# Scores of two attention heads issued together, their low-half passes on 64 rows each

## The chip, the cores and the metric

The kernel runs on one core of a Trainium2 chip. The metric is the time of one execution on the device, in microseconds (us). Differences of about 0.2% are what a measurement of this kernel can resolve.

## What is computed

One hybrid decoder layer over 512 tokens of width 1024 in float32: an mLSTM branch and a sparse-attention branch run in parallel on the normalised input, are merged by gates, and a gated convolution MLP follows. What matters here is the attention's selected and windowed part. With 8 query heads in 2 groups of 4, head width 64 and at most 8 selectable blocks of which 16 may be taken, both see all earlier keys, each with its own keys `ks`, `kw` and its own softmax:

```python
ps = masked_softmax(jnp.einsum('bghqd,bgqmd->bghqm', qb, ksel) * scale, smask)
o_slc = jnp.einsum('bghqm,bgqmd->bghqd', ps, vsel)
pw = masked_softmax(jnp.einsum('bghqd,bgkd->bghqk', qb, kwin) * scale, wmask)
o_win = jnp.einsum('bghqk,bgkd->bghqd', pw, vwin)
...
qk = jax.nn.silu(causal_dwconv(jnp.concatenate([mq, mk], axis=-1), m_conv_w, m_conv_b))
```

## The kernel before, in words

Matrix products with float32 accuracy are made of rounded float32 operands: each operand is split into a rounded high part and the low remainder, and a product is three passes, high by high, high by low and low by high. A pass is one TensorE instruction with its own weight load: up to 128 rows of contraction, 128 weight columns, 512 columns of the moving operand.

*Operands of the attention.* The head width is 64, so the array's 128 rows hold two things at once. `q_transposes` (L839) writes, for each head and each query tile of 128 tokens, a 128x128 block of `QS`: rows 0 to 63 the high part of q, rows 64 to 127 its low part (L850 subtracts on VectorE; L849 makes the rounded copy on ScalarE). The keys of both kinds stand twice, in rows 0 to 63 and again in 64 to 127, in `KKH` (high parts) and `KKL` (low parts).

*Scores.* `att_scores(i, h)` (L897) serves one head of query tile i, with n = i + 1 key tiles of 256 columns (both kinds). In blocks of up to 512 columns it issues the high pass (L906), on the last block the causal mask (L908), and the low pass (L909), all over 128 rows. One high pass so gives K_high times both parts of q, one low pass K_low times both. The scores go to `sp`, a tile of two PSUM banks, of which the pool has two (`psS`). VectorE then takes the maximum (L912).

*The rest of a head.* `att_exp` (L915) has ScalarE take the exponentials of the two kinds (L921) into a tile `P` of the pool `s4` (six slots); `att_scale` (L924) divides by the sum and multiplies by the gate on VectorE. `att_transposes` (L931) transposes up to four 128x128 blocks on TensorE into the only buffer `pt` and copies them back (L235 on VectorE or L233 on ScalarE, by the plan: in tile 3 the first four by VectorE, the second four by ScalarE; in tile 2 the other way round; tiles 0 and 1 have no second four). `att_pv` (L939) takes two heads and adds their outputs with passes of 64 weight columns (L947).

*The order* is written out by hand in `attention()` (L960): for the 32 (tile, head) pairs it issues the scores of the next head, then the transposes and, for odd heads, the output of the current one. At three points per head a `Filler` puts in work of the projections that remain (here `gm`, `mo`, `mqk`, `gn`: L488 to L490, three passes of 512 columns per step), by a budget in nanoseconds from the table `PLAN` (`f1`, `f2`, `f3`). For heads 4 to 7 the compressed branch of the next tile is put in at the end, and its output at the start of head 0. Each engine works its queue in the order of issue.

*The convolution.* `evac_conv` (L725) writes the convolved q and k of the mLSTM branch into `cv0` and `cv1`, two tiles of the pool `s4`; ScalarE starts each 512 columns and VectorE adds three taps (L732). The projection pages are 2048 columns wide, eight slots (`page`).

*The mLSTM part* that follows (`mls_s`, L1091) has passes over part of the rows: L1097 over rows 0 to 35, then L1105 to L1107 over 64 rows, the lower half for even heads, the upper half for odd ones.

Of the kernel before, what the change touches and what calls it, by code (L numbers as in the profile page):

```python
# [15 lines left out]
P = 128  # L16
# [112 lines left out]
def FL(key, default):  # L129
    return PLAN.get(key, default)  # L130
# [30 lines left out]
def body(ctx, tc, I, out, dbg=None):  # L161
# [26 lines left out]
    def sm(shape, name, bufs=2, dt=F32):  # L188
        return small.tile(shape, dt, name=name, tag=name, bufs=bufs)
# [16 lines left out]
    def s4(name, dt=F32):  # L206
        return ar.tile([P, 1024], dt, name=name, tag="s4", bufs=6)
# [4 lines left out]
    def psS(name):  # L212
        return ps.tile([P, 1024], F32, name=name, tag="s", bufs=2)
# [4 lines left out]
    def po(name):  # L218
        return ps.tile([P, 512], F32, name=name, tag="po", bufs=1)
# [503 lines left out]
        cp("e_mo", 0, T["mo"][:, m, :], a)  # L723

    def evac_conv(m, a):  # L725
        if m % 2 == 0:
            T[f"cv{m // 2}"] = s4(f"cv{m}")
        c = T[f"cv{m // 2}"][:, (m % 2) * 512:(m % 2) * 512 + 512]
        act.activation(c, a, AF.Identity, bias=col("m_conv_b", m), scale=col("m_conv_w", 12 + m))

        def tap(k):
            dve.scalar_tensor_tensor(c[:, k:], a[:, :S - k], col("m_conv_w", (3 - k) * 4 + m), c[:, k:],  # L732
                                     op0=ALU.mult, op1=ALU.add)
            if m == 3 and k == 3:
                done.add("CONV")

        for k in (1, 2, 3):
            after(k - 1, lambda k=k: tap(k))
# [88 lines left out]
    def qst(t):  # L827
        return T["QS"][t // 2][:, (t % 2) * 1024:(t % 2) * 1024 + 1024].rearrange("p (h c) -> p h c", h=8)
# [10 lines left out]
    def q_transposes(t, qdup):  # L839
        for hb in range(2):  # L840
            if hb:
                fill(FL("z6", 650))
            p = (po if hb else pt)(f"pq{t}{hb}")
            pv = p.rearrange("p (h c) -> p h c", h=4)
            for hh in range(4):
                h = hb * 4 + hh
                pe.transpose(pv[:, hh, :], qdup[:, h * P:(h + 1) * P], ident)
            d = qst(t)[:, hb * 4:hb * 4 + 4, :]
            act.activation(d, pv, AF.Copy)  # L849
            dve.tensor_sub(d[64:128], pv[64:128], d[64:128])  # L850

    def cmp_scores(i):
        q = qst(i)
        sp = psS(f"sc{i}")
        pe.matmul(sp[:, :512], identr, cmaskr[:, i:i + 1, :].to_broadcast([P, 8, 64]), start=True, stop=False)
        for h in range(8):
            pe.matmul(sp[:, h * 64:h * 64 + 64], q[:, h, :], kkc[:, h // 4].rearrange("p a n -> p (a n)"),
                      start=False, stop=(h == 7))
        sv = sp[:, :512].rearrange("p (h z n) -> p h z n", h=8, z=2)
        pc = vst[:, 1024:1792]  # L860
        raw = pc[:, 0:256].rearrange("p (h n) -> p h n", h=8)
        cp(f"e_sc{i}", 0, raw, sv[:, :, 1, :])
        s2 = pc[:, 256:512].rearrange("p (h n) -> p h n", h=8)
        dve.tensor_add(s2, sv[:, :, 0, :], raw)
        return pc
# [26 lines left out]
    def cmp_out(acc, pc):  # L892
        for pr in range(4):
            pe.matmul(acc[:, pr * P:(pr + 1) * P], vbd[:, pr // 2, pr % 2, :],
                      pc[:, 512 + (pr // 2) * P:512 + (pr // 2 + 1) * P], start=(pr == 0), stop=False)

    def att_scores(i, h):  # L897
        g = h // 4
        q = qst(i)[:, h, :]
        sp = psS(f"sp{i}_{h}")  # L900
        n = i + 1
        for b in range((n + 1) // 2):
            j1 = min(n, 2 * b + 2)
            w = (j1 - 2 * b) * 256
            o = sp[:, b * 512:b * 512 + w]
            pe.matmul(o, q, T["kkh"][:, g, 2 * b:j1].rearrange("p j y c -> p (j y c)"), start=True, stop=False)  # L906
            if j1 == n:
                pe.matmul(sp[:, i * 256:i * 256 + 256], identr, maskr, start=False, stop=False)  # L908
            pe.matmul(o, q, T["kkl"][:, g, 2 * b:j1].rearrange("p j y c -> p (j y c)"), start=False, stop=True)  # L909
        sv = sp[:, :n * 256].rearrange("p (j y c) -> p y j c", y=2, c=P)  # L910
        nmx = sm([P, 2], "nmx", 4)
        dve.tensor_reduce(nmx, sv, axis=AX.XY, op=ALU.max, negate=True)  # L912
        return sv, nmx

    def att_exp(i, h, sv, nmx):  # L915
        n = i + 1
        Pt = s4(f"P{i}_{h}")
        Pv = Pt[:, :n * 256].rearrange("p (j y c) -> p y j c", y=2, c=P)
        den = sm([P, 2], "aden", 4)
        for y in range(2):  # L920
            act.activation(Pv[:, y], sv[:, y], AF.Exp, bias=nmx[:, y:y + 1], accum_out=den[:, y:y + 1])  # L921
        return Pt, Pv, den

    def att_scale(i, h, Pv, den):  # L924
        gd = sm([P, 2], "agd", 4)
        dve.reciprocal(gd, den)
        dve.tensor_mul(gd, gd, gts[:, i, h * 3 + 1:h * 3 + 3])
        for y in range(2):
            (pool if FL(f"p_sc{i}{y}", 1) == 2 else dve).tensor_scalar(Pv[:, y], Pv[:, y], gd[:, y:y + 1], None, op0=ALU.mult)

    def att_transposes(i, h, b, Pt):  # L931

        nb = min(4, 2 * (i + 1) - 4 * b)
        p = pt(f"ptp{i}_{h}_{b}")
        for s in range(nb):
            pe.transpose(p[:, s * P:(s + 1) * P], Pt[:, (4 * b + s) * P:(4 * b + s + 1) * P], ident)  # L936
        cp(f"e_pt{i}{b}", 1 - b, Pt[:, b * 512:b * 512 + nb * P], p[:, :nb * P])

    def att_pv(i, h, PTs, acc):  # L939

        n = i + 1
        pr = h // 2
        for s in range(2 * n):
            j, y = s // 2, s % 2
            for z in range(2):
                g = (h + z) // 4
                pe.matmul(acc[z * 64:z * 64 + 64, pr * P:(pr + 1) * P], vv[:, y, j, g * 64:g * 64 + 64],  # L947
                          PTs[z][:, s * P:(s + 1) * P], start=False, stop=(h == 6 and s == 2 * n - 1))
# [9 lines left out]
        dve.tensor_sub(ol, av, oh)  # L958

    def attention():  # L960
        its = [(i, h) for i in range(NT) for h in range(8)]
        f1 = [FL(f"f1_{k}", v) for k, v in enumerate((1950, 1300, 1000, 1000)) for _ in range(8)]
        f2 = [FL(f"f2_{k}", v) for k, v in enumerate((0, 0, 1300, 1300)) for _ in range(8)]
        f3 = [FL(f"f3_{k}", v) for k, v in enumerate((650, 1000, 300, 300)) for _ in range(8)]
        pcs = {0: pc0}
        rows, step = rows_b(), None
        sv, nmx = att_scores(0, 0)
        Pt, Pv, den = att_exp(0, 0, sv, nmx)
        fill(FL("z7", 1950))
        att_scale(0, 0, Pv, den)  # L970
        acc = po("on0")
        cmp_out(acc, pcs[0])
        fill(FL("z9", 1300))
        for n, (i, h) in enumerate(its):
            nxt = its[n + 1] if n + 1 < len(its) else None
            if nxt:
                nsv, nnmx = att_scores(*nxt)
            fill(f1[n])
            if nxt and FL(f"q2_ex{i}", 0) == 0:
                nPt, nPv, nden = att_exp(*nxt, nsv, nnmx)  # L980
            if h == 0 and i:
                acc = po(f"on{i}")
                cmp_out(acc, pcs[i])
            nb = (i + 2) // 2
            att_transposes(i, h, 0, Pt)
            if nxt and FL(f"q2_ex{i}", 0) == 1:
                nPt, nPv, nden = att_exp(*nxt, nsv, nnmx)
            fill(f2[n])
            if nb > 1:
                att_transposes(i, h, 1, Pt)  # L990
            if nxt:
                att_scale(*nxt, nPv, nden)
            fill(f3[n])
            if h % 2:
                att_pv(i, h - 1, (prev, Pt), acc)
            prev = Pt
            if rows and n >= FL("q32_rb", 6) and (step != "R4" or h in (1, 2)):
                step = next(rows, "end")
                if step == "end":
                    rows = None  # L1000
                    done.add("ROWS")
            if i + 1 < NT:
                if h == 4:
                    pcs[i + 1] = cmp_scores(i + 1)
                elif h == 5:
                    cmp_exp(i + 1, pcs[i + 1])
                elif h == 6:
                    cmp_scale(i + 1, pcs[i + 1])
                elif h == 7:
                    cmp_transposes(i + 1, pcs[i + 1])  # L1010
            if h == 7:
                att_out(i, acc)
            if nxt:
                Pt, Pv, den = nPt, nPv, nden


    uoc = consts.tile([P, 40], F32, name="uoc")
# [634 lines left out]
```

## Time and profile before

| | |
|---|---|
| median of 3 runs | 787.01 us (786.48 to 788.13) |
| the profiled execution | 786.64 us, of which the span from the first to the last instruction is 784.8 us |
| TensorE matmul busy | 773.2 us (99% of the span) |
| TensorE weight loads busy | 640.5 us |
| VectorE, ScalarE, GpSimd busy | 466.5, 374.5, 211.3 us |
| the attention's scores to its last output | 120 to 276 us of the span |

Passes are pipelined: the bar of a pass is longer than the time it adds, so what a pass costs is read from one start to the next. In the time line each line is a start, a duration, the engine, the line of the kernel, the operation, the tile written and the tiles read, the form (rows*columns of the weights, then the moving operand), and in brackets how long the engine was idle before it and what it waited for.

### The profile page before, as it was taken

Reading aid. Unit: us, or ns where it says so; the run is one execution under the profiler, and the core shown is the slowest. Engines: PE = TensorE matmul, PEld = TensorE weight load, DVE = VectorE, ACT = ScalarE, POOL = GpSimd, SP = SyncE. Lnnn points to the kernel's source line nnn. Section 1 sums busy time; section 2 is a strip of 40 time slices with the busy share of each in tenths; the row PEclk is TensorE's granted clock in tenths of the full one; section 3 lists DMA queues with packets and bytes.
Section 4 is the critical chain, followed back from the end, with each engine's and each line's share of the span. In section 5 each row is a group of like instructions: output and inputs, shape, how many; then the busy total and the mean of one; then the engine's idle time right before and its main releaser. Section 6 shows DMA issues by size and latency. Waiting matters only on the chain.

```text
span 784.8 us, 10544 instructions
## 1 busy us (share of the span) xinstructions
PE 773.2 (99%) x4037; PEld 640.5 (82%) x4037; DVE 466.5 (59%) x823; ACT 374.5 (48%) x631; POOL 211.3 (27%) x221
## 2 busy tenths in 40 slices
PE   7999999999999999999999999999999999999998
PEld 5798778887888888888888988888888888888886
DVE  4576785677566754566627455545555454565865
ACT  6254536744665576475624253333433333455441
POOL 4420022121111113110110027755455443200700
PEclk9999999999999999999999999999999999999999
DMA  6984059756647466643588157664554534575472
GB/s 231 288 216 141 19 99 178 126 108 108 108 82 128 89 87 143 120 100 138 137 269 282 41 205 282 235 240 174 205 215 173 187 125 160 210 273 188 147 235 88
DMA packets 93892, 129.03 MB, mean 164 GB/s; under 512 B 6512, under 2 KB 72208, under 8 KB 92433
## 3 DMA queue, kind: packets, MB, share of 16 engines
q1 hardware_dynamic: 63054, 91.64, 35.0%
q0 software_dynamic: 30784, 36.70, 22.6%
q8 instruction: 32, 0.52, 0.3%
q14 instruction: 20, 0.16, 0.1%
q10 hardware_dynamic: 2, 0.00, 0.0%
HBM read 94.79 MB, written 15.73 MB: 141 GB/s over the span
## 4 chain that ended last, share of the span: by engine, by line
PE 90%; DVE 7%; ACT 2%; issue 1%; POOL 0%; DVEq 0%; POOLq 0%
PE ff L1368 10%; PE ff L1367 10%; PE ff L1369 10%; PE P L427 4%; PE P L428 4%; PE P L426 4%; PE on L947 2%; PE ptp L936 2%; PE wo L426 2%; PE wo L427 2%; PE wo L428 2%; PE gn L488 2%; PE gn L490 2%; PE gn L489 2%; PE gm L488 1%; PE gm L490 1%
## 5 line engine op out<-in xcount | busy, mean ns | idle before, releaser
L94 DVE TENSOR_TENSOR whl<-raw,whl 128x1024 fp32r<-128x1024 f32 (+1 forms) x108 | 136.5, 1276 | 148.7 <-ACT whl L88 148.7
L88 ACT ACTIVATE whl<-raw 128x1024 fp32r<-128x1024 f32 (+2 forms) x144 | 144.8, 1012 | 126.4 <-PE ff L1369 57.2
L1367 PE MATMUL ff<-h2H,whl 128*128 128x512 f32 (+1 forms) x384 | 142.8, 372 | 0.0
L1368 PE MATMUL ff<-h2L,whl 128*128 128x512 f32 (+1 forms) x384 | 142.6, 371 | 0.0
L1369 PE MATMUL ff<-h2H,whl 128*128 128x512 f32 (+1 forms) x384 | 142.6, 371 | 0.0
L92 POOL DMA_DIRECT2D whl<-raw x34 | 47.1, 1384 | 234.9 <-ACT whl L91 183.9
L1367 PEld LDWEIGHTS ff<-h2H,whl 128*128 128x128 f32 x384 | 72.3, 188 | 12.6
L1369 PEld LDWEIGHTS ff<-h2H,whl 128*128 128x128 f32 x384 | 72.3, 188 | 12.5
L1368 PEld LDWEIGHTS ff<-h2L,whl 128*128 128x128 f32 x384 | 72.4, 188 | 12.3
L921 ACT ACTIVATE P<-sp,nmx 128x128 f32<-128x128 f32 (+3 forms) x64 | 33.1, 524 | 36.9 <-DVE nmx L912 36.5
L1419 ACT ACTIVATE ct<-ct 128x512 f32<-128x512 f32 x22 | 13.9, 632 | 54.1 <-DVE ct L1417 54.1
L912 DVE TENSOR_REDUCE nmx<-sp 128x2 f32<-128x256 f32 (+3 forms) x32 | 26.2, 818 | 18.0 <-PE sp L909 17.9
L91 ACT ACTIVATE whl<-raw 128x1024 fp32r<-128x1024 f32 x34 | 35.7, 1049 | 0.0
L426 PE MATMUL P<-whl,g 128*128 128x512 f32 x88 | 34.2, 389 | 0.0
L427 PE MATMUL P<-whl,g 128*128 128x512 f32 x88 | 34.2, 389 | 0.0
L428 PE MATMUL P<-whl,g 128*128 128x512 f32 x88 | 34.2, 389 | 0.0
L1417 DVE SCALAR_TENSOR_TENSOR ct<-ff,vcol,ct 128x511 f32<-128x511 f32 (+1 forms) x44 | 32.7, 744 | 2.2 <-ACT ct L1415 1.4
L1425 ACT ACTIVATE g<-ct 128x512 fp32r<-128x512 f32 x22 | 13.9, 632 | 37.0 <-DVE ct L1429 21.9
L235 DVE COPY P<-ptp 128x256 f32<-128x256 f32 (+1 forms) x32 | 17.7, 554 | 18.6 <-PE ptp L936 18.4
L1426 DVE TENSOR_TENSOR g<-ct,g 128x512 fp32r<-128x512 f32 x22 | 15.4, 699 | 21.9 <-ACT g L1425 21.9
L488 PE MATMUL gm<-hTH,whl 128*128 128x512 f32 x64 | 26.6, 416 | 1.0 <-DVE mv L235 1.0
L427 PE MATMUL P<-whl,sb 128*128 128x512 f32 x66 | 25.9, 393 | 0.2
(400 smaller groups left out, 1783.0 us busy)
## 6 DMA issues: line engine op xcount, KB each, us to landing
raw<-in_ffn_w_up_dram SPq DMA_DIRECT2D x22, 1024.0 KB, 5.1
whl<-raw POOLq DMA_DIRECT2D x34, 512.0 KB, 5.7
raw<-in_w_in_dram SPq DMA_DIRECT2D x16, 1024.0 KB, 5.0
st<-in_ffn_w_down_dram SPq DMA_DIRECT2D x11, 1024.0 KB, 9.0
td<-st POOLq DMA_DIRECT2D x11, 1024.0 KB, 4.1
raw<-td SPq DMA_DIRECT2D x22, 512.0 KB, 5.2
raw<-in_ffn_w_down_dram SPq DMA_DIRECT2D x11, 512.0 KB, 4.8
raw<-in_w_out_dram SPq DMA_DIRECT2D x4, 1024.0 KB, 4.9
```

The lines of the kernel that those rows point to most:

```text
L88: nc.scalar.activation(h, src, AF.Copy)
L91: nc.scalar.activation(l, src, AF.Copy, scale=-1.0)
L92: nc.gpsimd.dma_start(l, src, accum_op=ALU.add)
L94: (nc.gpsimd if n in self.on_pool else nc.vector).tensor_sub(l, src, h)
L426: pe.matmul(o, aH, bH, start=start, stop=False)
L427: pe.matmul(o, aH, bL, start=False, stop=False)
L428: pe.matmul(o, aL, bH, start=False, stop=stop)
L488: pe.matmul(acc, H[:, k, :], hh, start=(k == 0), stop=False)
L921: act.activation(Pv[:, y], sv[:, y], AF.Exp, bias=nmx[:, y:y + 1], accum_out=den[:, y:y + 1])
L1367: pe.matmul(acc[:, a:b], H[:, k, :], hh, start=(k == 0), stop=False)
L1368: pe.matmul(acc[:, a:b], H[:, k, :], hl, start=False, stop=False)
L1369: pe.matmul(acc[:, a:b], L[:, k, :], hh, start=False, stop=(k == KD - 1))
```

## The change

Scores are issued for two neighbouring heads h and h+1 at a time. High passes and masks are as before, for one head and then for the other. The low passes now read 64 rows only: for the even head rows 0 to 63, for the odd head rows 64 to 127, and they are issued in turn, block by block. For this the odd heads' blocks of `QS` hold their halves the other way round (low part in rows 0 to 63, high part in rows 64 to 127), so that a low pass takes the high part of q alone; the product of the two low parts is left out. The two maxima follow behind both heads' passes. `attention()` runs over 16 pairs: scores of the next pair, then for each head of the current pair the same work and the same budgets as before. The exponentials of the next pair are issued one in each half. `cv0` and `cv1` become the halves of one page.

```diff
     def evac_conv(m, a):
-        if m % 2 == 0:
-            T[f"cv{m // 2}"] = s4(f"cv{m}")
+        if m == 0:
+            cvp = page("cv")
+            T["cv0"], T["cv1"] = cvp[:, 0:1024], cvp[:, 1024:2048]
...
             d = qst(t)[:, hb * 4:hb * 4 + 4, :]
             act.activation(d, pv, AF.Copy)
-            dve.tensor_sub(d[64:128], pv[64:128], d[64:128])
+
+            dz = d.rearrange("p (a z) c -> p z a c", z=2)
+            pz = pv.rearrange("p (a z) c -> p z a c", z=2)
+            dve.tensor_sub(dz[64:128, 0], pz[64:128, 0], dz[64:128, 0])
+            dve.tensor_sub(dz[0:64, 1], pz[0:64, 1], dz[0:64, 1])
...
     def att_scores(i, h):
+
         g = h // 4
-        q = qst(i)[:, h, :]
-        sp = psS(f"sp{i}_{h}")
         n = i + 1
-        for b in range((n + 1) // 2):
...
+        sp = [psS(f"sp{i}_{h + z}") for z in range(2)]
+        blk = [(2 * b, min(n, 2 * b + 2)) for b in range((n + 1) // 2)]
+        for z in range(2):
+            for j0, j1 in blk:
+                pe.matmul(sp[z][:, j0 * 256:j1 * 256], qst(i)[:, h + z, :],
+                          T["kkh"][:, g, j0:j1].rearrange("p j y c -> p (j y c)"), start=True, stop=False)
+            pe.matmul(sp[z][:, i * 256:i * 256 + 256], identr, maskr, start=False, stop=False)
+        for j0, j1 in blk:
+            for z in range(2):
+                r = slice(z * 64, z * 64 + 64)
+                pe.matmul(sp[z][:, j0 * 256:j1 * 256], qst(i)[r, h + z, :],
+                          T["kkl"][r, g, j0:j1].rearrange("p j y c -> p (j y c)"), start=False, stop=True)
+        res = []
+        for z in range(2):
+            sv = sp[z][:, :n * 256].rearrange("p (j y c) -> p y j c", y=2, c=P)
+            nmx = sm([P, 2], "nmx", 4)
+            dve.tensor_reduce(nmx, sv, axis=AX.XY, op=ALU.max, negate=True)
+            res.append((i, h + z, sv, nmx))
+        return res
...
+        for k, (i, h0) in enumerate(its):
+            nxt = its[k + 1] if k + 1 < len(its) else None
+            nsc, new = att_scores(*nxt) if nxt else None, []
+            for z in range(2):
+                h = h0 + z
+                fill(f1[i])
+                early = FL(f"q2_ex{i}", 0) == 0
+                if nxt and early:
+                    new.append(att_exp(*nsc[z]))
...
+                att_transposes(i, h, 0, cur[z][0])
+                if nxt and not early:
+                    new.append(att_exp(*nsc[z]))
+                fill(f2[i])
+                if i > 1:
+                    att_transposes(i, h, 1, cur[z][0])
+                if nxt:
+                    att_scale(nxt[0], nxt[1] + z, *new[z][1:])
+                fill(f3[i])
+                if z:
+                    att_pv(i, h0, (cur[0][0], cur[1][0]), acc)
```

## Rows read from the trace of the kernel before

**Rows 1.** The page: span, TensorE's busy time, and its granted clock in 40 slices.

```profile
span 784.8 us, 10544 instructions
...
PE 773.2 (99%) x4037; PEld 640.5 (82%) x4037; DVE 466.5 (59%) x823; ACT 374.5 (48%) x631; POOL 211.3 (27%) x221
...
PEclk9999999999999999999999999999999999999999
```

**Rows 2.** Busy time by stage, 119 to 275 us, summed (length, engines).

```profile
sum 156.00, PE 155.66 PEld 126.56 DVE 102.18 ACT 91.11 POOL 27.25; mean PE 38.92 PEld 31.64 DVE 25.54 ACT 22.78 POOL 6.81
```

**Rows 3.** Groups of TensorE by line and form: count, busy us, mean ns.

```profile
L909 PE MATMUL sp<-KKL,QS 128*128 128x512 f32 x32 | 12.6, 395 | 0.0
...
L909 PE MATMUL sp<-KKL,QS 128*128 128x256 f32 x16 | 4.5, 280 | 0.0
```

**Rows 4.** Time line of TensorE (start us, us), tile 3, 243 to 247 us.

```profile
243.28 0.39 PE L909 MATMUL sp<-KKL,QS 128*128 128x512 f32 x1
243.51 0.39 PE L906 MATMUL sp<-KKH,QS 128*128 128x512 f32 x1
...
244.09 0.39 PE L488 MATMUL mqk<-hTH,whl 128*128 128x512 f32 x1
...
246.59 0.60 PE L936 MATMUL ptp<-ident,P 128*128 128x128 f32 x4
```

**Rows 5.** Time line of TensorE, tile 0, passes of 256 columns.

```profile
126.56 0.28 PE L908 MATMUL sp<-maskr,identr 128*128 128x256 f32 x1
...
126.79 0.40 PE L488 MATMUL gm<-hTH,whl 128*128 128x512 f32 x1
```

**Rows 6.** Time line of TensorE, mLSTM head 0: into part-height passes and back.

```profile
288.52 0.39 PE L490 MATMUL gn<-hTH,whl 128*128 128x512 f32 x1
288.84 0.50 PE L1097 MATMUL mB<-mrowC,sel 36*128 36x512 f32 x1
289.18 0.40 PE L1105 MATMUL mA<-mq 64*128 64x512 f32 x1
...
291.00 0.28 PE L1107 MATMUL mB<-mq 64*128 64x256 f32 x1
291.20 0.50 PE L488 MATMUL gn<-hTH,whl 128*128 128x512 f32 x1
291.54 0.39 PE L489 MATMUL gn<-hTL,whl 128*128 128x512 f32 x1
```

**Rows 7.** Time line of TensorE, mLSTM head 1, whose L1105 reads the upper half.

```profile
300.48 0.49 PE L1097 MATMUL mB<-mrowC,sel 36*128 36x512 f32 x1
300.48 0.49 PE L1105 MATMUL mA<-mq 64*128 64x512 f32 x1
300.81 0.39 PE L1106 MATMUL mA<-mq 64*128 64x512 f32 x1
```

**Rows 8.** Time line of VectorE, tile 3: maximum and copy.

```profile
244.28 1.23 DVE L912 TENSOR_REDUCE nmx<-sp 128x2 f32<-128x1024 f32 x1 [2.71 <-PE sp L909]
245.43 0.68 DVE L235 COPY P<-ptp 128x512 f32<-128x512 f32 x1
```

**Rows 9.** Time lines of ScalarE and TensorE, odd head of tile 3.

```profile
250.96 0.68 ACT L921 ACTIVATE P<-sp,nmx 128x512 f32<-128x512 f32 x1
...
254.40 0.50 PE L906 MATMUL sp<-KKH,QS 128*128 128x512 f32 x1
```

**Rows 10.** Time line of TensorE, the wait inside an output of tile 1.

```profile
178.46 1.09 PE L947 MATMUL on<-P,vst 128*64 128x128 f32 x14 [0.34 <-DVE P L235]
```

**Rows 11.** The line L850: duration ns min/median/max, first and last start.

```profile
L850 DVE TENSOR_TENSOR QS<-pq,QS x8: 686/692/695, 101.0 to 119.9; 64x512 fp32r<-64x512 f32 x8
```

**Rows 12.** Time lines of VectorE and TensorE around the split of tile 2.

```profile
111.32 0.42 DVE L864 TENSOR_TENSOR vst<-sc,vst 128x256 f32<-128x256 f32 x1 [0.97 <-ACT vst L233]
113.70 1.30 DVE L850 TENSOR_TENSOR QS<-pq,QS 64x512 fp32r<-64x512 f32 x2 [1.96 <-ACT QS L849]
...
116.69 0.50 PE L488 MATMUL gm<-hTH,whl 128*128 128x512 f32 x1 [0.98 <-DVE mv L235]
```

More of the change, by code (lines that the diff above doesn't have):

```diff
@@ L898, in att_scores @@
         g = h // 4
-        q = qst(i)[:, h, :]
-        sp = psS(f"sp{i}_{h}")
         n = i + 1
-        for b in range((n + 1) // 2):
[L903 to L913, printed above, removed]
+        sp = [psS(f"sp{i}_{h + z}") for z in range(2)]
[17 more added lines that the diff above has]
+        return res
     def att_exp(i, h, sv, nmx):
@@ L960, in attention @@
     def attention():
[L961 to L964, printed above, removed]
+        its = [(i, h) for i in range(NT) for h in range(0, 8, 2)]
+        f1 = [FL(f"f1_{k}", v) for k, v in enumerate((1950, 1300, 1000, 1000))]
+        f2 = [FL(f"f2_{k}", v) for k, v in enumerate((0, 0, 1300, 1300))]
+        f3 = [FL(f"f3_{k}", v) for k, v in enumerate((650, 1000, 300, 300))]
         pcs = {0: pc0}
         rows, step = rows_b(), None
-        sv, nmx = att_scores(0, 0)
-        Pt, Pv, den = att_exp(0, 0, sv, nmx)
+        cur = [att_exp(*a) for a in att_scores(0, 0)]
         fill(FL("z7", 1950))
-        att_scale(0, 0, Pv, den)
+        for z in range(2):
+            att_scale(0, z, *cur[z][1:])
         acc = po("on0")
@@ L973, in attention @@
         fill(FL("z9", 1300))
[L974 to L1014, printed above, removed]
@@ new lines, in attention @@
+        for k, (i, h0) in enumerate(its):
+            nxt = its[k + 1] if k + 1 < len(its) else None
+            nsc, new = att_scores(*nxt) if nxt else None, []
+            for z in range(2):
+                h = h0 + z
[3 more added lines that the diff above has]
+                    new.append(att_exp(*nsc[z]))
+                if h == 0 and i:
+                    acc = po(f"on{i}")
+                    cmp_out(acc, pcs[i])
+                att_transposes(i, h, 0, cur[z][0])
[9 more added lines that the diff above has]
+                    att_pv(i, h0, (cur[0][0], cur[1][0]), acc)
+                if rows and i * 8 + h >= FL("q32_rb", 6) and (step != "R4" or h in (1, 2)):
+                    step = next(rows, "end")
+                    if step == "end":
+                        rows = None
+                        done.add("ROWS")
+                if i + 1 < NT:
+                    if h == 4:
+                        pcs[i + 1] = cmp_scores(i + 1)
+                    elif h == 5:
+                        cmp_exp(i + 1, pcs[i + 1])
+                    elif h == 6:
+                        cmp_scale(i + 1, pcs[i + 1])
+                    elif h == 7:
+                        cmp_transposes(i + 1, pcs[i + 1])
+                if h == 7:
+                    att_out(i, acc)
+            cur = new
```

## The prediction

> **What bounds the kernel now.** I read the page first: TensorE is busy for 773.2 of 784.8 us, no other engine for more than 60%, and the granted clock stands at nine tenths or more in all forty slices, which of the two levels is the 2.4 GHz one [rows 1]. A busy TensorE may still be a waiting one, so the second view is the table of stages over the attention, 119 to 275 us. There TensorE is idle for 0.34 us in 156 us, and VectorE and ScalarE have a third of the time free [rows 2]. So in this stretch a microsecond of TensorE work taken out, or added, moves everything behind it one for one, and little waiting is left to win. Behind the attention the page shows TensorE at nine tenths in every slice up to the end, so I let nothing be given back later. The third view is the time line of TensorE, where I take the distance from one start to the next and not the durations: a pass lasts 0.39 us by its bar, yet the next starts 0.23 us after it (243.28 to 243.51) [rows 4], since passes overlap in the pipeline. For 256 columns two passes take 0.23 us, 0.115 us each [rows 5].
>
> **The low passes.** They are 32 of 512 columns and 16 of 256 columns [rows 3]: 32 x 0.23 + 16 x 0.115 = 9.2 us. Each now uses all 128 rows; after the change two heads' passes stand on rows 0 to 63 and 64 to 127. Whether two such passes run at the same time the trace of before can show, because the mLSTM part (L1097, then L1105) does so by chance for every second head: a 36-row pass on the lower half is followed by a 64-row pass on the upper half. Both start at 300.48 and the third at 300.81 [rows 7], that is 0.33 us for loads and streams of two passes of 512 columns. Where both lie on the same half, one alone takes from 288.84 to 289.18, 0.34 us [rows 6]. So the overlap is whole, and the loads of the two halves overlap too; I charge 0.01 us for the second of a pair. That halves 9.2 us: a gain of 4.6 us, less 16 x 0.01.
>
> **What the halves cost.** The same place shows the price. Rows 6 are one excursion from 128-row passes to part-height ones and back. The pass ahead starts at 288.52 and its follower at 288.84: 0.32 where 0.23 is usual, 0.09 lost. The weight load of the first part-height pass starts with the pass itself instead of during its predecessor, and the next start is 0.34 later, 0.11 lost. On the way back, the last 256-column pass starts at 291.00 and the 128-row pass at 291.20: 0.20 where 0.115 is usual, 0.085 lost; and then 291.20 to 291.54, 0.11 lost. Together 0.39 us each time. There are four such excursions in the trace; the three others have the same 0.20 and 0.34 at their end. I read it as the array running empty at each change of height, with the next weights loaded only then. The Trainium skill has that rule (TensorEngine Tiling (Array Packing), Tiling Modes, Key Properties): changing the tiling mode drains the TensorE. It gives no price; the trace agrees with it, at 0.39 us for going and returning.
>
> The change makes 16 excursions, one for each pair of heads in each of four query tiles. How much an excursion halves depends on the tile:
> tile 0, one pair of 256 columns: before 0.23, after 0.115 + 0.40 = 0.52, a loss of 0.29;
> tile 1, one pair of 512: before 0.46, after 0.23 + 0.40 = 0.63, a loss of 0.17;
> tile 2, 512 and 256: before 0.69, after 0.345 + 0.40 = 0.75, a loss of 0.06;
> tile 3, twice 512: before 0.92, after 0.46 + 0.40 = 0.86, a gain of 0.06.
> The sum is a loss of 0.46, times four pairs: **1.9 us lost**. The high passes and the masks keep their number and height; that scores follow the 128x64 passes of the output once per pair is so before and after.
>
> **The new order.** Both heads' scores are now issued before the pair's work, so the maxima of both (L912) stand one behind the other on VectorE, ahead of the copy of the first transposes (L235). In tile 3 the copy is VectorE's, and the one buffer `pt` has to be free before the second transposes. Before, from the first filling pass after the scores (244.09) to the second transposes (246.59) TensorE has 2.50 us of work [rows 4]; with the 0.11 us of the slow return 2.6. VectorE's maximum and copy start 1.15 us apart, and the copy takes 0.68 [rows 8]. With two maxima, starting 0.12 us after the first filling pass, the copy ends at 0.12 + 2 x 1.15 + 0.68 = 3.1: TensorE waits for 0.5 us. This holds for the even heads 2 and 4 of tile 3 (for head 0 the compressed branch's passes stand in between, for head 6 no scores are left to issue): **1.0 us lost**. In tile 2 the first copy is ScalarE's; in tiles 0 and 1 there are no second transposes. Bounds: 0, if the first filling work covers it, and 3 us, if three VectorE passes of the convolution fall ahead of the copy too.
>
> The odd heads lose their maximum from VectorE. The one wait in the attention, 0.34 us of the output for such a copy (178.46) [rows 10], should go: **0.3 us won**. TensorE then goes straight on to the next scores.
>
> Both score buffers are taken by one pair, so the next pair's scores wait for both exponentials. The second one is queued in the odd half; before, an exponential in that place ended at 251.6 and the next scores began at 254.40 [rows 9]: nearly 3 us of cover. Cost nothing; without cover, the wait would be what ScalarE is late by. Four softmax tiles are live instead of three, and the convolution's two half pages leave that pool for a page of another, which the gate rows had left by then: six slots for at most five tiles, so no wait there.
>
> **The queries' split (L850).** Eight VectorE passes of 64x512 become sixteen of 64x256. One of the old ones takes 0.69 us [rows 11], two of them 1.30, so neighbours overlap by 0.08; a 256-wide pass with PSUM input takes 0.42 us [rows 12]. Four of these are 4 x 0.42 - 3 x 0.08 = 1.44: 0.14 us more per tile, 0.6 in all. Most of it lies beside filling passes, but after tile 2's split TensorE waits for VectorE's queue (0.98 us just before 116.69 [rows 12]), and the transposes wait for this buffer too, so I take **0.3 us lost**, between 0 and 0.6.
>
> **Sum.** 1.9 + 1.0 - 0.3 + 0.3 = 2.9 us slower. The profiled execution took 786.64 us, of which 784.8 are its span; it lies 0.4 us under the median of 787.01. 786.6 + 2.9 = **789.5 us**.
>
> **The rivals.** (1) *Changing the height costs nothing here, and the change does what its words promise.* Then 4.6 - 0.16 = 4.4 us are won, 1.0 of them lost at the copy: 786.6 - 4.4 + 1.0 = 783.2 us, faster. The place would be the step from the mask pass to the first low pass; it decides from 0.21 us per excursion downwards, where 16 of them cost no more than the overlap gives, less the 1.0. The Trainium skill speaks for it (the same page, Theoretical Speedup): with a contraction of 64 or less, up to twice the speed, and nothing is deducted there. Against it stand the exits in rows 6, which are changes from 64*128 to 128*128 exactly, four of four alike. Chance 0.13. (2) *The two halves don't overlap in this order.* Then the gain is gone and the switches stay: 16 x 0.39 = 6.2, and 786.6 + 6.2 + 1.0 = 793.8. Rows 7 speak against it, but show it for one pair only, not for pairs in sequence with reloads. Chance 0.07. (3) *The copy doesn't come late*, as VectorE takes the first maximum earlier or TensorE is itself later: 786.6 + 1.9 - 0.3 + 0.3 = 788.5. Chance 0.17. (4) *VectorE's queue becomes a bound in more places*, for convolution passes or two scalings fall ahead of a copy, in six pairs at some 0.5 us more: 792 to 793. Chance 0.11.
>
> **How the numbers follow.** My forecast, 789.5 us, has 0.52, with its own range 788.5 to 791. What a measurement of this kernel can tell from no change is about 0.2%, 1.6 us, so from 785.4 to 788.6 counts as the same. Faster is rival 1 alone, 0.13. The same is most of rival 3 (0.13) and the low end of the forecast (0.06): 0.19. Slower is the rest, 0.68. The range that leaves out rivals 1 and 2, 0.2 together, goes from 787.2 to 792.8.
>
> **What would show it.** Right: in each pair the two low passes start within 0.02 us of each other; the first starts about 0.2 us after a 256-column mask pass instead of 0.115 and is followed 0.34 us later; the filling pass after the scores starts late and takes 0.34 to its successor; TensorE's idle time in the attention is near 1 us, with the second transposes (L936) waiting for L235. Rival 1 would show 0.115 and 0.23 at these steps, rival 2 starts 0.23 us apart. Wrong in another way: idle TensorE at the scores, waiting for an exponential, or a gap for a page or a slot after the convolution moved.

## The result, and the profile after

The changed kernel takes 792.9 us (median of four runs, 792.6 to 794.1) against 787.1 us: 1.0074 times the time before, 95% interval 1.0059 to 1.0089, or 5.8 us more. The forecast was 789.5 us with a range up to 792.8. The direction and the mechanism named first (the halves cost more than their overlap gives) were right; the loss is twice the size.

The page of the changed kernel (span, busy time, granted clock), to hold against [rows 1]:

```profile
span 791.1 us, 10508 instructions
...
PE 778.3 (98%) x4037; PEld 639.3 (81%) x4037; DVE 468.2 (59%) x831; ACT 373.1 (47%) x631; POOL 211.2 (27%) x221
...
PEclk9999999999999999999999999999999999999999
```

The span is 6.3 us longer. All of it has come by the end of the attention: the last transposes of the softmax start at 279.7 instead of 273.4, and the first passes of the output projection at 394.0 instead of 387.7 (first and last start in the two lines, the kernel before and then the changed one). Behind that, both kernels run in step, so nothing is given back, as forecast.

```profile
L426 PE MATMUL wo<-whl,yH x64: 389/389/476, 387.7 to 432.3; 128*128 128x512 f32 x64
L426 PE MATMUL wo<-whl,yH x64: 389/389/476, 394.0 to 438.6; 128*128 128x512 f32 x64
```

First the passes themselves. The time line of TensorE in the changed kernel, first tile 0, then tile 3 (start, us, line, form; the numbers of lines are those of the changed kernel: L910 high pass, L912 mask, L916 low pass):

```profile
127.57 0.28 PE L912 MATMUL sp<-maskr,identr 128*128 128x256 f32 x1
127.78 0.38 PE L916 MATMUL sp<-KKL,QS 64*128 64x256 f32 x2
128.09 0.50 PE L488 MATMUL gm<-hTH,whl 128*128 128x512 f32 x1
128.43 0.39 PE L489 MATMUL gm<-hTL,whl 128*128 128x512 f32 x1
...
250.39 0.28 PE L912 MATMUL sp<-maskr,identr 128*128 128x256 f32 x1
250.60 0.73 PE L916 MATMUL sp<-KKL,QS 64*128 64x512 f32 x4
251.27 0.50 PE L488 MATMUL mqk<-hTH,whl 128*128 128x512 f32 x1
251.60 0.40 PE L489 MATMUL mqk<-hTL,whl 128*128 128x512 f32 x1
```

This is the excursion of [rows 6] again. The step from the mask to the first low pass is 0.21 us where 0.115 is usual; the filling pass follows 0.31 us after two low passes of 256 columns, which leaves 0.085 when 0.11 for the first load and 0.115 for one stream are taken off; its successor comes 0.34 us later instead of 0.23. Four low passes of 512 columns take 0.67 us in all, from 250.60 to 251.27: load 0.11, two streams of 0.23, and 0.09 to leave. So the halves do run at the same time, and going there and back costs the 0.39 us of the forecast.

Then the waits of TensorE in the changed kernel, 119 to 285 us (who waited for whom, us in total, times, longest):

```profile
PE ptp L947 <- DVE P L235: 0.6, 2, 0.3
PE ptp L947 <- ACT emc L1099: 0.5, 1, 0.5
PE sc L860 <- ACT P L932: 0.5, 2, 0.3
```

[Rows 2] had 0.34 us of idle time there in 156. The first of these lines was forecast, the other two not. `emc` is ScalarE's last read of the buffer `pt` for the mLSTM rows; `sc` is the compressed branch's scores, which need a score buffer. And ahead of the attention, the queries (first line) and the second head's first scores (the step from 123.05 to 123.41, where 0.115 us is usual):

```profile
115.50 0.63 PE L848 MATMUL pq<-ident,qdup 128*128 128x128 f32 x4 [1.57 <-DVE QS L855]
...
123.05 0.28 PE L912 MATMUL sp<-maskr,identr 128*128 128x256 f32 x1
123.41 0.38 PE L910 MATMUL sp<-KKH,QS 128*128 128x256 f32 x1
```

### The profile page after: what moved, and what is told of

Its sections match the earlier page's. It is cut to its first block, busy times and chain, and to the rows that moved or that the text cites. A ratio compares the mean times of both kernels' runs of the same rounds, so it can differ in the third digit from the quotient of the medians.

```text
span 791.1 us, 10508 instructions
## 1 busy us (share of the span) xinstructions
PE 778.3 (98%) x4037; PEld 639.3 (81%) x4037; DVE 468.2 (59%) x831; ACT 373.1 (47%) x631; POOL 211.2 (27%) x221
## 4 chain that ended last, share of the span: by engine, by line
PE 88%; DVE 7%; ACT 2%; DMA 1%; issue 1%; SPq 0%; DVEq 0%; ACTq 0%
PE ff L1379 10%; PE ff L1378 10%; PE ff L1377 10%; PE P L427 4%; PE P L428 4%; PE P L426 4%; PE on L958 2%; PE ptp L947 2%; PE wo L428 2%; PE wo L427 2%; PE wo L426 2%; PE gm L488 2%; PE gn L488 2%; PE gn L490 2%; PE gn L489 1%; PE gm L490 1%
## 5 line engine op out<-in xcount | busy, mean ns | idle before, releaser
L488 PE MATMUL gm<-hTH,whl 128*128 128x512 f32 x64 | 28.5, 445 | 0.7 <-DVE mv L235 0.7
L947 PE MATMUL ptp<-ident,P 128*128 128x128 f32 x160 | 25.5, 273 | 1.1 <-DVE P L235 0.6
```

Of the source, the lines that this page charges most:

```text
L488: pe.matmul(acc, H[:, k, :], hh, start=(k == 0), stop=False)
```

## The experiments

The trace offers three parts: the halves, the new order, and the queries' split. Theory A, formed from it, is that the halves lose 1.9 us as forecast, and that order and split lose the rest by waits; the rivals put the loss in one part alone, or hold that the halves win and something else loses more. All ratios are to the kernel before in the same sessions, with 95% intervals; a ratio of 1.001 is 0.8 us.

**Each part by itself.** *The split alone*, in the kernel before:

```diff
-            dve.tensor_sub(d[64:128], pv[64:128], d[64:128])
+            dz = d.rearrange("p (a z) c -> p z a c", z=2)
+            pz = pv.rearrange("p (a z) c -> p z a c", z=2)
+            dve.tensor_sub(dz[64:128, 0], pz[64:128, 0], dz[64:128, 0])
+            dve.tensor_sub(dz[0:64, 1], pz[0:64, 1], dz[0:64, 1])
```

> The kernel before with one part of the change alone: the queries' low parts are made in two passes of 64x256 per buffer, the odd heads' halves the other way round; scores, order and low passes over 128 rows stay. Theory A (the split is a large part of the loss, as TensorE waits at the fourth tile's transposes and then runs at the lower clock level for some us, as the trace of after shows at 113.6 to 121): 1 to 2.5 us slower than before, 788 to 789.5. Rival B (the split lies beside other work, the gap in that trace is chance): within 0.5 us of before, 787.0 to 787.5.

Measured: 1.0023 (1.0014 to 1.0032), 1.8 us. TensorE waits at the fourth tile's transposes, in the time line of this kernel:

```profile
115.82 0.63 PE L847 MATMUL pq<-ident,qdup 128*128 128x128 f32 x4 [1.59 <-DVE QS L853]
116.71 0.63 PE L847 MATMUL pq<-ident,qdup 128*128 128x128 f32 x4 [0.26 <-DVE QS L853]
```

Theory A's size holds and rival B is out. Theory A's reason, a fall of the clock, is neither shown nor excluded. In this trace the stage behind these waits has the granted clock 1.00 (last section). But this execution is the fastest of eleven, 787.98 us with a mean clock of 0.999; the ten others have mean clocks of 0.996 to 0.998 and took 788.3 to 790.1 us, and of the fifteen executions of the kernel before beside them six have 0.997 or 0.998. In the two traces, from the first query transposes to the first pass of the output projection, TensorE takes 291.2 us before and 292.1 here: 0.9 us, half of the 1.8.

*The order alone*, the changed kernel with

```diff
-                r = slice(z * 64, z * 64 + 64)
+                r = slice(0, 128)
```

and the old split:

> The changed kernel with the old split of the queries and with low passes over all 128 rows: only the order in pairs and the page for the convolution are new. Theory A (waits from the new order, for score buffers and for the copy of the transposes, cost about 1.6 us): 788.3 to 789.2. Rival C (the order costs nearly all of the 5.9 us): 791.5 to 793. Rival D (the halves win their 4.4 us, and the order loses more than that): 795 or more.

Measured: 1.0039 (1.0027 to 1.0052), 3.1 us. That is more than theory A and less than rival C, and rival D is out. TensorE's waits in this kernel, 119 to 285 us, which the kernel before has 0.34 us of:

```profile
PE sp L907 <- ACT mv L233: 1.1, 1, 1.1
PE sc L857 <- ACT P L929: 0.6, 2, 0.4
PE ptp L944 <- DVE P L235: 0.6, 2, 0.3
PE ptp L944 <- ACT emc L1096: 0.5, 1, 0.5
```

These are 2.8 us in six waits. A wait costs some 0.15 us more than its idle time: in the changed kernel the transposes at 254.38 were due at 253.89, 0.23 us after the pass ahead of them, so that 0.33 us of idle time cost 0.49 (those at 266.36 lost 0.48 for 0.31).

```profile
253.66 0.40 PE L490 MATMUL mqk<-hTH,whl 128*128 128x512 f32 x1
254.38 0.65 PE L947 MATMUL ptp<-ident,P 128*128 128x128 f32 x4 [0.33 <-DVE P L235]
```

So 2.8 + 6 x 0.15 - (0.34 + 0.15), the last for the wait of [rows 10] that is gone, gives 3.2 us, and 3.1 were measured. The first of the four lines of waits is the largest and new to me: the V projection's last accumulators lie in a score buffer until ScalarE has copied them, and a pair needs both score buffers at once.

*The split's part taken out of the changed kernel*, by transposing the four even heads into one buffer and the four odd ones into the other:

```diff
-                h = hb * 4 + hh
+                h = 2 * hh + hb
...
-            d = qst(t)[:, hb * 4:hb * 4 + 4, :]
+            d = qst(t).rearrange("p (a z) c -> p z a c", z=2)[:, hb]
...
+            lo = slice(64, 128) if hb == 0 else slice(0, 64)
+            dve.tensor_sub(d[lo], pv[lo], d[lo])
```

> The changed kernel with the query transposes grouped by parity: one buffer takes the four even heads, the other the four odd ones, so that one VectorE pass of 64x512 per buffer makes the low parts, as before the change. Theory A: the split's part comes off, 1 to 2.5 us faster than the changed kernel, 790.4 to 792, and TensorE's granted clock stays at the upper level at 113 to 121 us. Rival B: no change, 792.5 to 793.3.

Measured: 1.0064 (1.0051 to 1.0076), 792.25 us: 0.8 us less than the changed kernel by the ratios, between the two expectations and with intervals that overlap, so this run alone decides nothing, and that the split costs less inside the change than alone is not shown. In the traces, over the stretch named above, it is the other way round: 295.8 us here and 297.3 in the changed kernel, 1.5 us. The granted clock is 1.00 here from 113 to 121 us, as theory A expected. The wait of the second head's first scores only changes its place: with the split they lose 0.25 us (123.05 to 123.41, less 0.115), without it they wait 1.2 us, both times until ScalarE copies V out of the score buffer:

```profile
122.71 0.38 PE L908 MATMUL sp<-KKH,QS 128*128 128x256 f32 x1 [1.21 <-ACT mv L233]
```

With the split that copy comes 1.3 us later, counted from the first query transposes (26.0 us instead of 24.7). The two copies, the changed kernel's first:

```profile
122.75 0.60 ACT L233 ACTIVATE mv<-aVs 128x512 f32<-128x512 f32 x1 [1.92 <-DVE mv L235]
122.06 0.60 ACT L233 ACTIVATE mv<-aVs 128x512 f32<-128x512 f32 x1 [1.58 <-DVE mv L235]
```

Against order_only this run differs in the halves, and in which heads share a transpose buffer: 1.0064 to 1.0039, **2.0 us for the halves**, with 1.9 forecast (1.8 us between the two traces). Each of the two intervals is about 1 us wide either way.

**The price of an excursion.** The kernel before, with the low pass of each head over rows 0 to 63 in its old place:

```diff
-            pe.matmul(o, q, T["kkl"][:, g, 2 * b:j1].rearrange("p j y c -> p (j y c)"), start=False, stop=True)
+            pe.matmul(o, q[0:64], T["kkl"][0:64, g, 2 * b:j1].rearrange("p j y c -> p (j y c)"), start=False, stop=True)
```

> The kernel before with each low pass over rows 0 to 63 alone, head by head in the old order: 48 excursions from 128 rows to 64 and back (one per head in query tiles 0 and 1, two per head in tiles 2 and 3), with no second half beside them. It leaves out the product of the two low parts, as the changed kernel does. Theory A (0.39 us per excursion): 48 x 0.395 = 19.0 us slower, 806. Rival E (a change of height costs nothing here): 787, as before. If only the one way costs, some 797.

Measured: 805.7 us, 1.0227 (1.0214 to 1.0241), 17.9 us or 0.37 us for each of 48. The time line of one head in tile 3:

```profile
250.66 0.39 PE L490 MATMUL mqk<-hTH,whl 128*128 128x512 f32 x1
250.89 0.40 PE L906 MATMUL sp<-KKH,QS 128*128 128x512 f32 x1
251.21 0.50 PE L909 MATMUL sp<-KKL,QS 64*128 64x512 f32 x1
251.64 0.50 PE L906 MATMUL sp<-KKH,QS 128*128 128x512 f32 x1
251.98 0.28 PE L908 MATMUL sp<-maskr,identr 128*128 128x256 f32 x1
```

The steps are 0.32 into the low pass, 0.43 over it and 0.34 over the pass behind it, where each would be 0.23: 0.40 together. Rival E is out, and so is the case that only the one way costs (797).

**The waits taken away one by one.** First the V copy alone, on the run with the new order:

```diff
-    "e_mv2": 1,
+    "e_mv2": 0,
```

> The run with the new order alone (790.4), and one entry of the plan changed: the third part of the V projection is copied out of the score buffer by ScalarE instead of VectorE, so that ScalarE's fourth copy doesn't wait for VectorE and the second score buffer is free earlier. Theory A (of the order's 3.1 us, 1.1 are the second head's first scores waiting for that buffer): 789.2 to 789.6. Rival G (with this wait gone TensorE waits elsewhere): 790.2 to 790.6.

Measured: 789.3 us, 1.0020 (1.0011 to 1.0029), 1.5 us less than the order alone, with 1.1 expected (1.08 us of idle time and 0.15 by the rule above would be 1.2). Its trace has no wait for `mv` left at the scores.

Then all of them:

```diff
-    "e_mv2": 1,
+    "e_mv2": 0,
...
-    "e_pt30": 1, "e_pt31": 0,
+    "e_pt30": 0, "e_pt31": 1,
...
-    "q2_ex3": 0,
+    "q2_ex3": 1,
...
+                if h == 5 and i + 1 < NT:
+                    pcs[i + 1] = cmp_scores(i + 1)
                 fill(f3[i])
...
-                    if h == 4:
-                        pcs[i + 1] = cmp_scores(i + 1)
-                    elif h == 5:
+                    if h == 5:
...
-                if rows and i * 8 + h >= FL("q32_rb", 6) and (step != "R4" or h in (1, 2)):
+                if rows and i * 8 + h >= FL("q32_rb", 6) and (step != "R4" or h in (0, 1)):
```

> The run with the new order alone, with each wait that its trace shows taken away: the V copy as in order_mv; the compressed branch's scores issued one head later, when the first score buffer has long been free; the mLSTM rows' transposes one head earlier; in the fourth query tile the first transposes' copy on ScalarE ahead of the exponentials and the second's on VectorE. Theory A (the waits are the whole of the 3.1 us): 786.8 to 787.8, as before the change or up to 0.5 faster. Rival G (they come back elsewhere): over 788.8.

Measured: 787.5 us, 1.0000 (0.9991 to 1.0008), and TensorE waits for nothing from 119 to 285 us. Rival G is out. So the order's 3.1 us were these waits, to within the 0.7 us of the interval. The remedies were not tried on the kernel before; its trace has only the one wait of 0.34 us there for them to win.

**The halves without the waits.** The new order with the same remedies, with the change's halves and the parity buffers that they need:

> The changed kernel with its halves in the changed order (high passes, masks, then low passes in turn), parity buffers, and the four waits taken away as in order_fixed. What is left against order_fixed (787.5, ratio 1.000) is the halves alone. Theory A (16 excursions at 0.39 us against an overlap worth 4.4 us): 1.9 us slower than order_fixed, 788.9 to 789.6. Rival D (without waits the halves win): 783 to 786.

Measured: 789.1 us, 1.0026 (1.0017 to 1.0035). Against order_fixed the halves lose 2.0 us again (1.7 us between the traces), this time with no wait at TensorE from 119 to 285 us that could hide or make a difference. Rival D is out.

Is there an overlap at all? order_fixed, with both heads' low passes on rows 0 to 63 (so the queries lie as before the change, and no parity buffers are needed):

```diff
-                r = slice(z * 64, z * 64 + 64)
+                r = slice(0, 64)
```

> order_fixed with every low pass over rows 0 to 63, for both heads of a pair: the same 16 excursions and the same low passes in turn, but both on one half of the array, so nothing can overlap. It leaves out the product of the two low parts, as the changed kernel does. Theory A (the overlap is worth half of 9.2 us less 0.2): 4.4 us slower than change_no_waits, that is 16 x 0.39 = 6.3 us slower than before, 793.3 to 794. Rival 2 of the forecast (the halves never overlapped): the same as change_no_waits.

Measured: 793.6 us, 1.0077 (1.0064 to 1.0090), 4.0 us more than change_no_waits by the ratios and 4.5 by the medians. The low passes of a pair in tile 3, in this kernel:

```profile
250.70 0.28 PE L909 MATMUL sp<-maskr,identr 128*128 128x256 f32 x1
250.91 1.17 PE L913 MATMUL sp<-KKL,QS 64*128 64x512 f32 x4
252.01 0.50 PE L488 MATMUL mqk<-hTH,whl 128*128 128x512 f32 x1
252.35 0.40 PE L489 MATMUL mqk<-hTL,whl 128*128 128x512 f32 x1
```

Four passes take 1.10 us here and 0.67 where they alternate between the halves. Rival 2 of the forecast is out: the overlap is worth what was expected of it, 4.4 us. Without it, the 16 excursions cost 6.1 us over order_fixed (1.0077 to 1.0000), 0.38 us each.

**Fewer changes of form.** The outputs (128x64, 64 weight columns) stand before most scores, and behind them the form changes anyway. On the parity run, the low passes are issued first:

```diff
+        for j0, j1 in blk:
+            for z in range(2):
+                r = slice(z * 64, z * 64 + 64)
+                pe.matmul(sp[z][:, j0 * 256:j1 * 256], qst(i)[r, h + z, :],
+                          T["kkl"][r, g, j0:j1].rearrange("p j y c -> p (j y c)"), start=True, stop=False)
         for z in range(2):
             for j0, j1 in blk:
                 pe.matmul(sp[z][:, j0 * 256:j1 * 256], qst(i)[:, h + z, :],
-                          T["kkh"][:, g, j0:j1].rearrange("p j y c -> p (j y c)"), start=True, stop=False)
-            pe.matmul(sp[z][:, i * 256:i * 256 + 256], identr, maskr, start=False, stop=False)
-        for j0, j1 in blk:
...
+                          T["kkh"][:, g, j0:j1].rearrange("p j y c -> p (j y c)"), start=False, stop=j1 < n)
+            pe.matmul(sp[z][:, i * 256:i * 256 + 256], identr, maskr, start=False, stop=True)
```

> The run with the query buffers grouped by parity (792.25), with the low passes of both heads issued ahead of the high passes and masks. The score passes mostly follow the outputs, which have 64 weight columns and end in a change of form anyway, so each pair has one change less: 128 to 128x64 to 64x128 to 128, instead of going back to 128 in between. Theory A (each change costs 0.2 us whichever forms it joins): 12 to 16 pairs x 0.2 = 2.4 to 3.2 us faster, 789.0 to 789.9. Rival F (the cost belongs to the part-height passes themselves, so the place does not matter): 792.

Measured: 788.3 us, 1.0011 (1.0002 to 1.0020), 4.2 us less than the parity run by the ratios, 3.1 us in the traces over the stretch named above. Rival F is out; theory A is 1 us short of the ratios. The time line of tile 0 shows one change less:

```profile
131.37 0.66 PE L956 MATMUL on<-P,vst 128*64 128x128 f32 x8
131.95 0.38 PE L909 MATMUL sp<-KKL,QS 64*128 64x256 f32 x2
132.27 0.39 PE L913 MATMUL sp<-KKH,QS 128*128 128x256 f32 x1
132.49 0.29 PE L915 MATMUL sp<-maskr,identr 128*128 128x256 f32 x1
...
132.85 0.39 PE L488 MATMUL gm<-hTH,whl 128*128 128x512 f32 x1
133.08 0.40 PE L489 MATMUL gm<-hTL,whl 128*128 128x512 f32 x1
```

From 131.95 to 132.85 the scores take 0.90 us, and the filling pass is followed after 0.23 us; in the changed kernel the pair at the same place takes 0.99 (133.47 to 134.46), and its filling pass is followed after 0.34, so 0.20 us are saved here. Part of the further microsecond is a wait that is gone: `ptp` no longer waits for VectorE's copy in this trace (0.6 us idle before, in two places), which fits the first head's last pass now coming earlier than the second's; that this is the reason is argued and not tried by itself.

**All remedies together**, low passes over 128 rows in tile 0, where an overlap saves least:

```diff
-                r = slice(z * 64, z * 64 + 64)
+                r = slice(z * 64, z * 64 + 64) if i else slice(0, 128)
```

> All remedies in one: parity buffers, low passes first, the four waits taken away as in order_fixed, and in the first query tile, whose passes are short, low passes over 128 rows as before. Theory A: 787.2 for the order, minus for each pair the overlap's gain less one change of 0.2 us: tile 1 0.02, tile 2 0.13, tile 3 0.25, four pairs each, 1.6 together: 785.2 to 786.2, faster than both kernels. Rival F: 788 or more.

Measured: 785.8 us, 0.9980 (0.9970 to 0.9990): **1.6 us faster than the kernel before** (0.8 to 2.4 by the interval) and some 7 us faster than the changed one. A part of the 1.6 may be the clock: all nine executions have a mean clock of 1.000, and the ten of the kernel before with that clock average 786.8 us, 1.0 more. In the traces, over the stretch named above, it takes 290.0 us instead of 291.2. Its page:

```profile
span 784.2 us, 10493 instructions
...
PE 773.9 (99%) x4037; PEld 638.1 (81%) x4037; DVE 466.0 (59%) x822; ACT 372.9 (48%) x632; POOL 210.9 (27%) x221
```

## Why the prediction was right and wrong

*What bounds the kernel, and that nothing is given back*: right, by the equal shifts above. (The page's last slice of TensorE is at eight tenths, not nine, in both kernels.)

*The halves*: right in mechanism and size. 1.9 us lost were forecast (the four terms add up to 1.84), 2.0 were measured twice (parity_buffers against order_only, change_no_waits against order_fixed). The overlap, read from a single pair of passes [rows 7], was whole; the 0.39 us per excursion [rows 6] came out at 0.37 over 48 and 0.38 over 16. The Trainium skill (TensorEngine Tiling (Array Packing), Tiling Modes, Key Properties) says both things, that tiles work independently and that a change of mode drains the engine, and the runs agree with both: 0.67 us for four alternating passes instead of 1.10, and 0.37 us per excursion. The same page of the Trainium skill (Overview, Theoretical Speedup) has up to twice the speed for a contraction of 64 or less, and two streams at a time are what these four passes show. But the overlap of an excursion is 0.115, 0.23, 0.345 and 0.46 us in the four tiles, by the steps of 0.115 and 0.23 us, and only the last of these earns the 0.39 back.

*The new order*: this is the step that failed. 1.0 - 0.3 = 0.7 us were forecast, 3.1 us were measured. The two late copies in tile 3 came as forecast, at heads 2 and 4, 0.49 and 0.48 us. The sentence "Both score buffers are taken by one pair ... Cost nothing" is what was wrong. It looked only at the next pair, where [rows 9] gave nearly 3 us of cover, and not at the other users of the same two buffers: the V projection's accumulators ahead of the first pair, which are now in the way of the first pair's second head (1.1 us, the largest of the waits; before, that head's scores came only after 2 us of filling work, 120.80 to 122.89), and the compressed branch's scores in the middle of a pair (0.6 us in two places). The buffer `pt` had one more user too, the mLSTM rows (0.5 us). Each of these is an edit costed at nothing whose cover was not named for every user of the buffer. With these waits taken away the loss is gone (order_fixed, 1.0000). The 0.3 us that the forecast took off, for the wait of [rows 10], were right: that wait is in no trace with the new order.

*The queries' split*: a term too small. 0.3 us were forecast, with 0.6 as the upper bound; 1.8 us were measured alone, and 0.8 within the change, which its interval doesn't tell from 1.8 or from nothing. I had taken off an overlap that the small passes mostly don't have: they start 0.44, 0.45 and 0.44 apart where each lasts 0.43. The time line of VectorE in the changed kernel:

```profile
114.50 0.43 DVE L854 TENSOR_TENSOR QS<-pq,QS 64x256 fp32r<-64x256 f32 x1 [1.95 <-ACT QS L850]
114.94 0.42 DVE L855 TENSOR_TENSOR QS<-pq,QS 64x256 fp32r<-64x256 f32 x1
115.39 0.43 DVE L854 TENSOR_TENSOR QS<-pq,QS 64x256 fp32r<-64x256 f32 x1
115.83 0.42 DVE L855 TENSOR_TENSOR QS<-pq,QS 64x256 fp32r<-64x256 f32 x1
```

From the first of them to VectorE's next pass are 1.67 us where it was 1.33, so 0.34 us more per tile instead of the 0.14 of the forecast. In the first tile, the kernel before and then split_only:

```profile
101.01 1.30 DVE L850 TENSOR_TENSOR QS<-pq,QS 64x512 fp32r<-64x512 f32 x2
102.34 0.69 DVE L680 TENSOR_TENSOR qraw<-qraw,rrs 128x512 f32<-128x512 f32 x1
...
101.51 0.43 DVE L852 TENSOR_TENSOR QS<-pq,QS 64x256 fp32r<-64x256 f32 x1
103.18 0.67 DVE L680 TENSOR_TENSOR qraw<-qraw,rrs 128x512 f32<-128x512 f32 x1
```

And the delays of four tiles add up along one chain of VectorE and ScalarE, which releases `pq` and the V copy: 4 x 0.34 is 1.4 us, and 1.3 were found at the V copy. I had put most of them beside filling passes. Why the median of split_only shows 1.8 us and its trace 0.9 stays open; the lower mean clock of the other ten executions is one candidate, and none of them was traced.

*The sum*: 2.0 + 3.1 + 0.8 = 5.9 us, for 5.8 measured. That is no check of its own, since the three are the steps from one kernel to the next (before, order_only, parity_buffers, changed); what checks them is that the halves lose the same 2.0 us without the waits, and that the order loses nothing without them. *The rivals*: rival 1 and rival 2 fell with the 0.21 and 0.31 steps and with one_half_twice, rival 3 with the two late copies. Rival 4, VectorE's queue as a bound in more places, was the nearest in time (792 to 793), but by luck: it wanted the copy late in six pairs, at 0.5 us more each, and the changed kernel's trace has it late in the two places of the forecast and in no other.

What stays open: how the 4.2 us of low_first divide between the change of form and the late copies, why order_mv gained 1.5 and not 1.1 us (their intervals allow it), and what the split costs with the clock at its upper level throughout.

## What to carry to other kernels

Splitting passes over the array's halves pays when the overlap it gives is longer than the change there and back, here 0.39 us; so put such passes where the form changes anyway (low_first: 4.2 us, of them a part by a wait that went), and leave short ones alone; that many of them in one place pay follows from the same numbers but was not tried. When work is issued for two items at a time, list every user of each buffer that is now taken twice, before and behind the loop and in the middle of it, and not only the next round of the loop. A trace often holds a few instances of what a change will do, and reading two of them here gave the loss by the halves as 1.9 us, where 2.0 were measured, before anything was built.

## What was not expected of the hardware

In the profiled execution of the changed kernel TensorE's granted clock fell, after it had waited 1.57, 0.26 and 0.67 us at the queries' transposes and the first `gm` pass, and passes of 512 columns then started 0.43 us apart until 120.84, the 1.2 GHz level, before 0.23 again. The tables by stage (length, busy time of PE, PEld, DVE, ACT, POOL, granted clock, DMA), first the changed kernel, then split_only, which has the same waits (1.59, 0.26 and 0.67):

```profile
117.00:121.00 4.00, 3.33 (x9) 2.65 (x9) 2.60 (x9) 3.77 (x6) 1.32 (x1) 0.57 0.90 114
```

```profile
117.30:121.30 4.00, 3.33 (x15) 2.72 (x15) 2.60 (x9) 3.77 (x6) 1.31 (x1) 1.00 0.90 115
```

Nine passes began in the one stretch and fifteen in the other. In the changed kernel the fall probably cost little: its other executions, two of them with a mean clock of 1.000, took as long, and the stretch ended in front of the V copy, for which TensorE has to wait without the slow passes (1.21 us in parity_buffers, 0.25 us here). In split_only, which has the old order, no such wait follows, and ten of its eleven executions have mean clocks of 0.996 to 0.998; there a fall may well cost time, and no run here shows how much. A fall of the clock that ends in a wait should not be put down as a cause before an execution without it has been seen; and one trace without a fall doesn't show that the other executions had none.
